# Hybrid decoder layer on one NeuronCore: key weights of the memory packed block by block, small loads behind them, the inverse in pieces, up-projections later

## The chip, the cores and the metric

One NeuronCore of a Trainium2 chip runs the whole program. The metric is the device time of that core in microseconds (us), as the median of the timed runs.

## What is computed

One step of a decoder layer for 320 tokens (256 of a prompt, 64 of a sample). Everything is fp32.

```python
xn = rmsnorm(x);  p = xn @ w_in        # 82 blocks of 128 columns: RWKV r, k, v, low-rank parts, SWA, memory q, gates
A  = rwkv7(p)          # 12 heads of 64: decay from tanh(low rank) @ up, delta rule, group norm, times g
B  = sliding_window_attention(p);  C = cross_attention(p, K(mem), V(mem))
K, V = rmsnorm(mem) @ w_mem_kv         # 256 tokens of memory
h  = x + rmsnorm((sum_i sigmoid(gate_i) * (o_i @ w_br_i)) @ w_o)
y  = h + rmsnorm((gelu(conv(z_gate)) * z_val) @ w_ffn_down)
```

## The kernel before

**Matmuls.** Each fp32 weight tile is split into a high part `wh` (a cast on ACT) and a low part `wl` (a subtraction on DVE), each fp32r. The activations are split too (`XH`, `XL`). One 128x128 weight tile costs three matmuls (`mm3`, L101 to L103): `wh` with `XH`, `wh` with `XL`, `wl` with `XH`. The text calls these three one k-step. A projection to 128 columns takes 16 k-steps over the 2048 inputs. Its weight comes in two chunks of 8 tiles (512 KB), and each chunk has one ACT cast (L356) and one DVE subtraction (L357, 128x1024).

**Opening stage.** The parameters `prm` are loaded first, as one transfer. Then nine blocks `KR` of the memory and of its key weights follow (`kload`, L197; `kprep`, L204): the first two hold one tile of 128 inputs, the others two. A block of key weights is gathered from four column tiles, so a partition gets four runs of 512 B or 1 KB. In `kprep` ACT casts the weight (L191), DVE or ACT makes `MH`, DVE makes `ML` (L215) and `wl` (L217), and PE multiplies into `psk`. Then come the value weights (`vload`, `vprep`, `vmm`), between them the RMS norm of `x`: `normed` (L253) takes the inverse norm `SX`, which ACT has copied out of PSUM (L304), and for each of 16 tiles DVE makes `xn` (L255), ACT casts it to `XH` (L256), POOL subtracts to `XL` (L257). The order on PE, ACT, DVE and POOL is that of the program text in this stage.

**RWKV stage.** A queue of projections (`push`, `prefetch`, `step`) gives PE its k-steps; weights are requested four chunks ahead and split two chunks ahead. Between k-steps the planner `pump` lets small threads issue their instructions. Its clock advances 0.405 per k-step, and a number that a thread yields is a pause on this clock. Three kinds of threads work on six head pairs `hp`: `early(hp)` (L487) does the up-projection of decay and `a` (L493, two matmuls into two buffers of the PSUM pool `pea`), a normalised key (L518 to L525), the scores (L544) and the products `AU` and `AP` (L601, copied by DVE at L602); `inverse(hp)` (L611) inverts blocks of 32 on DVE in one loop of pieces of 8; `late(hp)` (L653) solves, walks over the chunks (L724) and does the group norm: mean, variance (`rstd`, L129, then `rsv` on DVE, a power on POOL, `rex` on DVE at L138), spread back (L146), times `rn` (L760), gate up-projection (`psg`, L764) and product (L766). In this stage only PE keeps the order of the planner; the other engines' instructions are placed by a scheduler in the order in which they were issued, as they become ready. The pool `pea` (tag `sm`) has two buffers, so L493 must wait until both earlier tiles in it have been read.

**Later stages**: gates, attention, `w_o` and the ConvGLU, all k-steps; the change touches none of them.

Of the kernel before, what the change touches and what calls it, by code (L numbers as in the profile page):

```python
# [9 lines left out]
F32 = mybir.dt.float32  # L10
# [6 lines left out]
T = 320  # L17
# [9 lines left out]
HOP = 1.2  # L27
HV = (0, 1) * 8
TAIL = ((0, 1, 0), (11, 1, 1), (1, 2, 0), (3, 2, 0), (12, 1, 1), (5, 2, 0), (13, 1, 1), (7, 2, 0), (14, 1, 1), (9, 2, 0), (15, 1, 1))
E0 = 9.0  # L30
KKN, TRN_V, PRE = 3.2, 3.6, 4.8
NRM = (4, 3, 2)
UPQ = 7
RST = 2.5
SLV = 2.4
NI_LAT = 6.0
BLK_LAT = 6.0
IT_LAT = 8.0
SOFT = 3.5
SSOFT2, TRN2 = 9.0, 3.6  # L40
# [22 lines left out]
def tile_hybrid_step(ctx: ExitStack, tc: tile.TileContext, i, o):  # L63
    nc = tc.nc
# [35 lines left out]
    def mm3(ps, h, l, xh, xl, start, stop):  # L100
        PE.matmul(ps, h, xh, start=start, stop=False)  # L101
        PE.matmul(ps, h, xl, start=False, stop=False)  # L102
        PE.matmul(ps, l, xh, start=False, stop=stop)  # L103
# [37 lines left out]
    def spread(psum, ex, nh, tbs=TB):  # L141
        ps = psum.tile([128, 512], F32, tag="sm", name="sm")
        n = 0
        for j, (_, c0, c1) in enumerate(tbs):
            lhs = ex[:, j:j + 1].to_broadcast([128, 128]) if nh == 1 else ex[:, j, :]
            PE.matmul(ps[:, n:n + c1 - c0], lhs, C["ident"][:, c0:c1], start=True, stop=True)  # L146
            n += c1 - c0
        return ps[:, :n]
# [2 lines left out]
        A.copy(out=h, in_=src)  # L151
        V.tensor_sub(out=l, in0=src, in1=h.bitcast(F32))

    nc.sync.dma_start(out=prm, in_=i["param"])

    xst = ctx.enter_context(ExitStack())
    xp = xst.enter_context(tc.tile_pool(name="xp", bufs=1, side="left"))
# [10 lines left out]
    with tc.tile_pool(name="st", bufs=1, side="right") as st, tc.tile_pool(name="st2", bufs=3, side="right") as st2, \  # L168
# [12 lines left out]
        def load(dst, src):  # L181
            tc.keep_in_program_order(nc.sync.dma_start(out=dst, in_=src))
            return dst
# [13 lines left out]
        def kload(k0, kn):  # L197
            m2 = load(st2.tile([128, 2, 256], F32, tag="m2", name="m2", bufs=4)[:, :kn], i["memT"][:, k0:k0 + kn, :])
            r = raw(nq[0])[:, :512 * kn]
            nq[0] += 1  # L200
            load(r.rearrange("p (m c) -> p m c", m=4), i["wmk"][:, :, 128 * k0:128 * (k0 + kn)].rearrange("m p c -> p m c"))
            return m2, r

        def kprep(k0, kn, m2, r):  # L204
# [48 lines left out]
        def normed(k):  # L253
            t = st2.tile([128, T], F32, tag="xn", name="xn")
            V.scalar_tensor_tensor(out=t, in0=xf[:, k, :], scalar=col("g_pre", k), in1=SX, op0=ALU.mult, op1=ALU.mult)  # L255
            A.copy(out=XH[:, k, :], in_=t)  # L256
            G.tensor_sub(out=XL[:, k, :], in0=t, in1=XH[:, k, :].bitcast(F32))  # L257

        ld = [kload(*KR[q]) for q in range(3)]
        for q in range(9):  # L260
            if q + 3 < 9:
                ld.append(kload(*KR[q + 3]))
                if q == 3:
                    load(cst, i["const"])
            kprep(*KR[q], *ld[q])
        vr, vw = [], []

# [19 lines left out]
        xsquare(2)  # L287
        vmm(1)
        SM = st.tile([128, 256], F32, name="SM")
        SX = st.tile([128, T], F32, name="SX")  # L290
        sm = spread(smp, smt, 1, tbs=TB[:2])
        xsquare(3)
        A.copy(out=SM, in_=sm)
# [4 lines left out]
        vload(6)  # L298
        vprep(4)
        vmm(3, (0,))  # L300
        sx = spread(smp, xr, 1)
        vload(7)
        vprep(5)
        A.copy(out=SX, in_=sx)  # L304
        vmm(3, (1,))
        vmm(4)
        nk = 0
# [27 lines left out]

    def push(src, nk, xsel, done, ready=None):
        ch = [[src[:, k * 128:min(k + 8, nk) * 128], min(8, nk - k), None, None] for k in range(0, nk, 8)]
        jobs.append(dict(nk=nk, xs=xsel, done=done, ready=ready, ch=ch, k=0, ps=None))

    def prefetch():  # L340
        upcoming = []
# [18 lines left out]
    def step():  # L360
        if not jobs or (jobs[0]["ready"] is not None and not jobs[0]["ready"]()):
            return False
        j = jobs[0]
        k = j["k"]
        if k % 8 == 0:
            prefetch()
        if j["ps"] is None:
            j["ps"] = big.tile([128, 512], F32, tag="big", name="bigps")[:, :T]
        h, l = j["ch"][k // 8][3]
        xh, xl = j["xs"](k)  # L370
        js = slice((k % 8) * 128, (k % 8 + 1) * 128)
        mm3(j["ps"], h[:, js], l[:, js], xh, xl, k == 0, k == j["nk"] - 1)
        j["k"] += 1
        if j["k"] == j["nk"]:
            jobs.popleft()
            j["done"](j["ps"])
        return True

    def spawn(gen):
# [26 lines left out]
    with tc.tile_pool(name="rws", bufs=1, side="right") as rws, tc.tile_pool(name="rwp", bufs=2, side="right") as rwp, \  # L406
# [64 lines left out]
        def rw_done(hp, n, tix):  # L471
            def done(ps):
                rkv[hp, n] = rwt.tile([128, T], F32, tag="rkv", name="rkv", bufs=6)
                shifted(ps, tix, rkv[hp, n])
            return done
# [11 lines left out]
        def early(hp):  # L487
            cs = slice(hp * 128, hp * 128 + 128)
            yield lambda: "lora0" in state
            yield E0 if hp == 0 else 0.0  # L490
            psz, psa = (pea.tile([128, 512], F32, tag="sm", name="sm")[:, :T] for _ in range(2))
            for ps, rs in ((psz, slice(0, 64)), (psa, slice(64, 128))):
                PE.matmul(ps, lw[rs, 0, cs], lora[0][rs], start=True, stop=True)  # L493
# [104 lines left out]
            for c in range(10):  # L598
                for h in range(2):
                    r0, r1 = slice(64 * h + 32 * (c % 2), 64 * h + 32 * (c % 2) + 32), slice(64 * h + 32, 64 * h + 64)  # L600
                    PE.matmul(ps1[r0, c // 2, :], BT[r1, c, 96:128], AU[r1, c, 64:128], start=True, stop=True)  # L601
            V.tensor_copy(out=AP[:, :, 64:128], in_=ps1[:, 0:5])  # L602
            psb = pea.tile([128, 512], F32, tag="sm", name="sm")[:, :T]
            PE.matmul(psb, C["bones"], sr, start=True, stop=True)
            yield lambda: state["or"] >= hp - 1
# [5 lines left out]
        def inverse(hp, NI, it):  # L611
            yield lambda: state["inv"] == hp
            yield NI_LAT
            R = rw1.tile([128, 6, 32], F32, tag="R", name="R")
            W = rw1.tile([128, 6, 8], F32, tag="W", name="W")
            prod = rw1.tile([128, 576], F32, tag="prod", name="prod")
            NF = NI[0:120].rearrange("p j t -> p (j t)")
            for t in range(1, 8):
                nd = bass.AP(tensor=NF.tensor, offset=NF.offset + t, ap=[NF.ap[0], [264, 4], [0, t], [32, t]])
                pv = prod[0:120, 0:4 * t * t].rearrange("p (b i j) -> p b i j", i=t, j=t)  # L620
                V.tensor_mul(out=pv, in0=DI[0:120, :, 0:t, 0:t], in1=nd)
                V.tensor_reduce(out=DI[0:120, :, 0:t, t], in_=pv, axis=AX.X, op=ALU.add)
            yield 4.0
            for b in range(4):
                w = E[0:120, :, 0:8]
                if b:
                    nj = 8 * b
                    stp = 6 if b == 1 else 3
                    for i0 in range(0, 6, stp):
                        pv = prod[0:120, 0:stp * 8 * nj].rearrange("p (i t j) -> p i t j", t=8, j=nj)  # L630
                        V.tensor_mul(out=pv, in0=R[0:120, i0:i0 + stp, 0:nj].unsqueeze(2).to_broadcast([120, stp, 8, nj]),
                                     in1=NI[0:120, 0:nj, nj:nj + 8].rearrange("p j t -> p t j").unsqueeze(1).to_broadcast([120, stp, 8, nj]))
                        V.tensor_reduce(out=W[0:120, i0:i0 + stp, :], in_=pv, axis=AX.X, op=ALU.add)
                    w = W[0:120]
                    V.tensor_add(out=w, in0=w, in1=E[0:120, :, nj:nj + 8])
                pv = prod[0:120, 0:384].rearrange("p (i t j) -> p i t j", t=8, j=8)
                V.tensor_mul(out=pv, in0=w.unsqueeze(2).to_broadcast([120, 6, 8, 8]),
                             in1=DI[0:120, b].rearrange("p j t -> p t j").unsqueeze(1).to_broadcast([120, 6, 8, 8]))
                V.tensor_reduce(out=R[0:120, :, 8 * b:8 * b + 8], in_=pv, axis=AX.X, op=ALU.add)
                yield BLK_LAT  # L640
            sc2 = dsc.tile([20, 36, 32], F32, tag="sc2", name="sc2")
            nc.gpsimd.dma_start(out=sc2.rearrange("u i t -> (u i) t").rearrange("(p i) t -> p i t", i=6), in_=R[0:120])
            yield lambda: state["late"] >= hp - 1
            IT = its[hp % 2]
            for h in range(2):
                for q in range(2):
                    nc.gpsimd.dma_start(out=IT[64 * h + 32 * q:64 * h + 32 * q + 32, :, 32 * q:32 * q + 32],
                                        in_=sc2[10 * h + q:10 * h + 10:2, 0:32, :].rearrange("u j t -> j u t"))
            state["inv"] = hp + 1
            yield IT_LAT  # L650
            it[0] = IT
# [120 lines left out]
                yield from early(hp)  # L772

        fill = [(QKV, j, O_Q + j if j < 6 else O_K + j - 6) for j in range(10)] + [(MQ, j, O_MQ + j) for j in range(4)]
        for j in range(2):
            push(i["win"][O_LORA + j], 16, xs, lora_done(j))
        for hp in range(6):
            for n, nm, tix in ((1, "k", 6 + hp), (0, "r", hp), (2, "v", 12 + hp)):
                push(i["win"][O_RW + 3 * hp + n], 16, xs, rw_done(hp, nm, tix))
            for _ in range(FILL[hp]):  # L780
                dst, j, mt = fill.pop()
                push(i["win"][mt], 16, xs, fill_done(dst, j))
# [367 lines left out]
    with tc.tile_pool(name="ff", bufs=1, side="left") as ff, tc.tile_pool(name="fft", bufs=2, side="left") as fft, \  # L1150
# [6 lines left out]
        j = 0  # L1157
# [210 lines left out]
```

## Time and profile before

| | |
|---|---|
| runs | 2054.89, 2054.66, 2051.91 us; median 2054.66 |
| profiled execution | 2050.91 us, its span 2049.1 us |
| PE busy | 1988.0 us (97%), mean granted clock 0.987 |
| DVE, ACT, POOL busy | 1226.4, 821.6, 203.1 us |
| read from HBM | 293.53 MB, mean 148 GB/s |

The profiled execution lies 3.75 us under the median. Its time is 1.8 us more than its span, the time around the first and the last instruction. Busy times add up over the program and say little of one stage; the waits of an engine and the chosen stretches of time (below) show where PE stood.

### The profile page before, as it was taken

How to read it: one execution, taken by the hardware profiler on the slowest of the kernel's cores; microseconds unless marked ns; L12 is line 12 of the kernel's file. 1: busy time of each engine (PE TensorE's matmuls, PEld its weight loads, DVE VectorE, ACT ScalarE, POOL GpSimd, SP SyncE). 2: the span in 40 equal slices, each digit the busy share in tenths (PEclk: the TensorE clock that was granted, in tenths of full speed). 3: DMA queues.
4: the chain of work that ended last, by engine and by line, in shares of the span. 5: the costliest groups of instructions: out<-in, count | busy, mean ns of one | idle time of the engine just before them, and what ended most of it. 6: DMA issues, size and time to landing. Idle time of an engine off the chain costs nothing.

```text
span 2049.1 us, 36434 instructions
## 1 busy us (share of the span) xinstructions
PE 1988.0 (97%) x14923; PEld 1929.5 (94%) x14923; DVE 1226.4 (60%) x2048; ACT 821.6 (40%) x1306; POOL 203.1 (10%) x452
## 2 busy tenths in 40 slices
PE   7999898989999999999999999999999999999997
PEld 7888797889998999999999999999999999999997
DVE  7788777875457754444547653555555555455456
ACT  5533443433443433333445443433343333334235
POOL 4511231121200000000100100000000000000001
PEclk9999999999999999999999999999999999999999
DMA  7533343334545444544553444445444444444443
GB/s 272 171 127 101 108 126 93 104 111 128 193 162 164 139 129 150 161 150 154 194 173 116 141 151 148 152 159 181 145 153 148 151 151 148 151 148 155 145 139 127
DMA packets 93000, 303.28 MB, mean 148 GB/s; under 512 B 11356, under 2 KB 17654, under 8 KB 92816
## 3 DMA queue, kind: packets, MB, share of 16 engines
q1 hardware_dynamic: 83232, 273.42, 40.2%
q0 software_dynamic: 8880, 26.71, 3.9%
q8 instruction: 117, 1.92, 0.4%
q10 hardware_dynamic: 720, 0.82, 0.1%
q14 instruction: 51, 0.42, 0.1%
HBM read 293.53 MB, written 9.34 MB: 148 GB/s over the span
## 4 chain that ended last, share of the span: by engine, by line
PE 60%; issue 5%; POOL 1%; DVE 0%; ACT 0%; POOLq 0%; DVEq 0%
PE bigps L101 19%; PE bigps L102 19%; PE bigps L103 19%; PE bigps L1139 0%; PE bigps L1137 0%; PE bigps L1140 0%; POOL yacc L1227 0%; POOL merged L1062 0%; POOL yacc L1228 0%; DVE MG L813 0%; PE sm L146 0%; PE sm L870 0%; POOL rsr L1087 0%; PE psos L1021 0%; PE sm L1212 0%
## 5 line engine op out<-in xcount | busy, mean ns | idle before, releaser
L101 PE MATMUL bigps<-XH,wh 128*128 128x320 f32 x2656 | 843.6, 318 | 1.0 <-ACT gt L830 0.5
L103 PE MATMUL bigps<-XH,wl 128*128 128x320 f32 x2656 | 824.8, 311 | 2.1 <-DVE wl L357 2.1
L102 PE MATMUL bigps<-XL,wh 128*128 128x320 f32 x2656 | 825.0, 311 | 1.6 <-POOL XL L257 1.5
L97 DVE TENSOR_TENSOR wl<-raw,wh 128x1024 fp32r<-128x1024 f32 (+1 forms) x299 | 357.4, 1196 | 275.7 <-ACT wh L96 275.4
L101 PEld LDWEIGHTS bigps<-XH,wh 128*128 128x128 f32 x2656 | 502.4, 189 | 17.4 <-issue 12.7
L96 ACT CAST wh<-raw 128x1024 fp32r<-128x1024 f32 (+1 forms) x299 | 306.4, 1025 | 519.6 <-PE bigps L102 396.2
L102 PEld LDWEIGHTS bigps<-XL,wh 128*128 128x128 f32 x2656 | 502.7, 189 | 4.1 <-POOL XL L257 2.4
L103 PEld LDWEIGHTS bigps<-XH,wl 128*128 128x128 f32 x2656 | 502.1, 189 | 2.6 <-DVE wl L357 2.6
L357 DVE TENSOR_TENSOR wl<-raw,wh 128x1024 fp32r<-128x1024 f32 (+2 forms) x212 | 245.2, 1157 | 197.4 <-ACT wh L356 193.8
L356 ACT CAST wh<-raw 128x1024 fp32r<-128x1024 f32 (+2 forms) x212 | 208.3, 983 | 304.5 <-PE bigps L102 251.6
L102 PE MATMUL bigps<-fl,wh 128*128 128x320 f32 x704 | 217.5, 309 | 0.0
L101 PE MATMUL bigps<-fh,wh 128*128 128x320 f32 x704 | 217.4, 309 | 0.0
L103 PE MATMUL bigps<-fh,wl 128*128 128x320 f32 x704 | 217.4, 309 | 0.0
L101 PEld LDWEIGHTS bigps<-fh,wh 128*128 128x128 f32 x704 | 132.2, 188 | 0.2 <-ACT fh L151 0.2
L102 PEld LDWEIGHTS bigps<-fl,wh 128*128 128x128 f32 x704 | 132.2, 188 | 0.1
L103 PEld LDWEIGHTS bigps<-fh,wl 128*128 128x128 f32 x704 | 132.2, 188 | 0.0
L1196 DVE TENSOR_TENSOR yacc<-yacc,bigps 128x320 f32<-128x320 f32 x80 | 38.9, 487 | 84.1 <-PE bigps L103 84.0
L1170 POOL COPY cout<-zp 128x9 f32<-128x9 f32 x88 | 15.4, 205 | 731.6 <-DVE zp L1167 731.6
L101 PE MATMUL bigps<-MG,wh 128*128 128x320 f32 x208 | 64.4, 309 | 0.3 <-ACT MG L812 0.3
L103 PE MATMUL bigps<-MG,wl 128*128 128x320 f32 x208 | 64.3, 309 | 0.0
L102 PE MATMUL bigps<-MG,wh 128*128 128x320 f32 x208 | 64.3, 309 | 0.0
L1166 DVE TENSOR_TENSOR zp<-bigps,S 128x256 f32<-128x256 f32 x44 | 18.7, 425 | 56.7 <-PE bigps L103 56.7
(404 smaller groups left out, 2367.9 us busy)
## 6 DMA issues: line engine op xcount, KB each, us to landing
raw<-in_wup SPq DMA_DIRECT2D x176, 512.0 KB, 3.5
raw<-in_win SPq DMA_DIRECT2D x164, 512.0 KB, 3.6
raw<-in_wdn SPq DMA_DIRECT2D x80, 512.0 KB, 3.2
raw<-in_wo SPq DMA_DIRECT2D x32, 512.0 KB, 3.7
raw<-in_wbr_rw SPq DMA_DIRECT2D x16, 384.0 KB, 3.3
raw<-in_wbr_sw SPq DMA_DIRECT2D x16, 384.0 KB, 3.1
ck<-in_cmk POOLq DMA_DIRECT2D x8, 512.0 KB, 4.7
cv<-in_cmv POOLq DMA_DIRECT2D x8, 512.0 KB, 3.7
```

Of the source, the lines that this page charges most:

```text
L96: A.copy(out=h, in_=raw)
L97: V.tensor_sub(out=l, in0=raw, in1=h.bitcast(F32))
L101: PE.matmul(ps, h, xh, start=start, stop=False)
L102: PE.matmul(ps, h, xl, start=False, stop=False)
L103: PE.matmul(ps, l, xh, start=False, stop=stop)
L356: A.copy(out=h, in_=c[2])
L357: V.tensor_sub(out=l, in0=c[2], in1=h.bitcast(F32))
L1166: V.tensor_mul(out=zp[:, 2:258], in0=psz[:, 0:TP], in1=S2[:, 0:TP])
L1170: G.tensor_copy(out=cout[:, j, :, e], in_=zp[:, 256 + e:337 + e:10])
L1196: V.tensor_add(out=yacc[:, m, :], in0=yacc[:, m, :], in1=ps)
```

## The change

1. Parameters: only their first 32 columns (the gains of the two norms) are loaded ahead of the key weights; the other columns and the constants go behind the ninth block of them.
2. The host packs the key weights block by block, so that one block is one run of 2 KB or 4 KB per partition.
3. `SX` stays in PSUM. The subtraction to `XL` of tiles 2, 5, 8, 11 and 14 goes from POOL to DVE, one tile later.
4. The first low-rank projection and the first key projection alternate chunk by chunk (`push_pair`).
5. `E1`: the up-projection of `hp` 1 to 5 pauses 5.0 on the planner's clock; before, it had no pause. The copy of `AP` goes from DVE to ACT.
6. `RST`, the pause between variance and spread, is 3.4 and was 2.5.
7. The inverse pauses after `t` of 4 and of 7 and after each off-diagonal piece (2.4), and 3.0 instead of 6.0 after each block.

```diff
-E0 = 9.0
+E0, E1 = 9.0, 5.0
 KKN, TRN_V, PRE = 3.2, 3.6, 4.8
 NRM = (4, 3, 2)
 UPQ = 7
-RST = 2.5
+RST = 3.4
 SLV = 2.4
 NI_LAT = 6.0
-BLK_LAT = 6.0
+PIECE, BLK_LAT = 2.4, 3.0
...
-    nc.sync.dma_start(out=prm, in_=i["param"])
+    nc.sync.dma_start(out=prm[:, 0:32], in_=i["param"][:, 0:32])
...
-            load(r.rearrange("p (m c) -> p m c", m=4), i["wmk"][:, :, 128 * k0:128 * (k0 + kn)].rearrange("m p c -> p m c"))
+            load(r, i["wmk"][:, 512 * k0:512 * (k0 + kn)])
             return m2, r
...
             A.copy(out=XH[:, k, :], in_=t)
+            if k % 3 == 2:
+                low.append((k, t))
+                return
+            if low:
+                k1, t1 = low.pop()
+                V.tensor_sub(out=XL[:, k1, :], in0=t1, in1=XH[:, k1, :].bitcast(F32))
             G.tensor_sub(out=XL[:, k, :], in0=t, in1=XH[:, k, :].bitcast(F32))
+
+        low = []
 
         ld = [kload(*KR[q]) for q in range(3)]
         for q in range(9):
             if q + 3 < 9:
                 ld.append(kload(*KR[q + 3]))
-                if q == 3:
+                if q == 5:
                     load(cst, i["const"])
+                    load(prm[:, 32:], i["param"][:, 32:])
...
             kprep(*KR[q], *ld[q])
         vr, vw = [], []
 
...
-        SX = st.tile([128, T], F32, name="SX")
...
-        sx = spread(smp, xr, 1)
+        SX = spread(smp, xr, 1)
         vload(7)
         vprep(5)
-        A.copy(out=SX, in_=sx)
         vmm(3, (1,))
         vmm(4)
         nk = 0
...
     def push(src, nk, xsel, done, ready=None):
         ch = [[src[:, k * 128:min(k + 8, nk) * 128], min(8, nk - k), None, None] for k in range(0, nk, 8)]
-        jobs.append(dict(nk=nk, xs=xsel, done=done, ready=ready, ch=ch, k=0, ps=None))
+        jobs.append(dict(nk=nk, xs=xsel, done=[done], ready=ready, ch=ch, k=0, ps=[None]))
+
+    def push_pair(srcs, xsel, dones):
+        ch = [[src[:, k * 128:(k + 8) * 128], 8, None, None] for k in (0, 8) for src in srcs]
+        jobs.append(dict(nk=32, xs=xsel, done=dones, ready=None, ch=ch, k=0, ps=[None, None]))
 
...
-        if j["ps"] is None:
-            j["ps"] = big.tile([128, 512], F32, tag="big", name="bigps")[:, :T]
+        nl = len(j["ps"])
+        q, kk = k // 8 % nl, k // (8 * nl) * 8 + k % 8
+        if j["ps"][q] is None:
+            j["ps"][q] = big.tile([128, 512], F32, tag="big", name="bigps")[:, :T]
         h, l = j["ch"][k // 8][3]
-        xh, xl = j["xs"](k)
+        xh, xl = j["xs"](kk)
         js = slice((k % 8) * 128, (k % 8 + 1) * 128)
-        mm3(j["ps"], h[:, js], l[:, js], xh, xl, k == 0, k == j["nk"] - 1)
+        last = kk == j["nk"] // nl - 1
+        mm3(j["ps"][q], h[:, js], l[:, js], xh, xl, kk == 0, last)
         j["k"] += 1
         if j["k"] == j["nk"]:
             jobs.popleft()
-            j["done"](j["ps"])
+        if last:
+            j["done"][q](j["ps"][q])
         return True
...
             yield lambda: "lora0" in state
-            yield E0 if hp == 0 else 0.0
+            yield E0 if hp == 0 else E1
...
-            V.tensor_copy(out=AP[:, :, 64:128], in_=ps1[:, 0:5])
+            A.copy(out=AP[:, :, 64:128], in_=ps1[:, 0:5])
...
                 pv = prod[0:120, 0:4 * t * t].rearrange("p (b i j) -> p b i j", i=t, j=t)
                 V.tensor_mul(out=pv, in0=DI[0:120, :, 0:t, 0:t], in1=nd)
                 V.tensor_reduce(out=DI[0:120, :, 0:t, t], in_=pv, axis=AX.X, op=ALU.add)
-            yield 4.0
+                if t in (4, 7):
+                    yield PIECE
...
                         V.tensor_mul(out=pv, in0=R[0:120, i0:i0 + stp, 0:nj].unsqueeze(2).to_broadcast([120, stp, 8, nj]),
                                      in1=NI[0:120, 0:nj, nj:nj + 8].rearrange("p j t -> p t j").unsqueeze(1).to_broadcast([120, stp, 8, nj]))
                         V.tensor_reduce(out=W[0:120, i0:i0 + stp, :], in_=pv, axis=AX.X, op=ALU.add)
+                        yield PIECE
                     w = W[0:120]
...
-        for j in range(2):
-            push(i["win"][O_LORA + j], 16, xs, lora_done(j))
         for hp in range(6):
-            for n, nm, tix in ((1, "k", 6 + hp), (0, "r", hp), (2, "v", 12 + hp)):
-                push(i["win"][O_RW + 3 * hp + n], 16, xs, rw_done(hp, nm, tix))
+            three = [(O_RW + 3 * hp + n, rw_done(hp, nm, tix)) for n, nm, tix in ((1, "k", 6 + hp), (0, "r", hp), (2, "v", 12 + hp))]
+            if hp == 0:
+                push_pair((i["win"][O_LORA], i["win"][three[0][0]]), xs, [lora_done(0), three[0][1]])
+                push(i["win"][O_LORA + 1], 16, xs, lora_done(1))
+                three = three[1:]
+            for mt, done in three:
+                push(i["win"][mt], 16, xs, done)
...
     wmk = mtiles(np.asarray(w_mem_kv)[:, :512])
+    wmk = A(np.concatenate([wmk[:, :, 128 * k:128 * (k + n)].transpose(1, 0, 2).reshape(128, 512 * n)
+                            for k, n in [(0, 1), (1, 1)] + [(k, 2) for k in range(2, 16, 2)]], 1))
```

PE at the end of `early` of the second head pair and the start of the third one's. L601 and L604 are the last products of `early`, L493 the up-projection, L724 one step of the walk over chunks. Before:

```order
L601 MATMUL sm<-AU,BT 32x64 x20
L604 MATMUL sm<-rkv,cst 128x320
L493 MATMUL sm<-lora_755,lw 128x320 [waits DVE_49] x2
L101 MATMUL bigps<-XH,wh 128x320
L102 MATMUL bigps<-XL,wh 128x320
L103 MATMUL bigps<-XH,wl 128x320
L724 MATMUL psb<-SA,AB 128x64 [waits Activation_49]
```

After the change (L616, L619, L508 and L741 are the same instructions). Between L619 and L508 stand thirteen k-steps and four steps of the walk; the first k-step and one step of the walk are shown:

```order
L616 MATMUL sm<-AU,BT 32x64 x12
L619 MATMUL sm<-rkv,cst 128x320
L101 MATMUL bigps<-XH,wh 128x320
L102 MATMUL bigps<-XL,wh 128x320
L103 MATMUL bigps<-XH,wl 128x320
...
L741 MATMUL psb<-SA,AB 128x64 [waits Activation_49]
...
L508 MATMUL sm<-lora_754,lw 128x320 [waits PE_49]
L508 MATMUL sm<-lora_754,lw 128x320 [waits DVE_49]
```

The up-projection moved from directly behind L604 to 13 k-steps behind it.

DVE at the same place: the inverse (L637 to L633), then the copy of `AP` and the product `bonus`. Before:

```order
L637 TENSOR_TENSOR prod<-rcst 120x384 [waits DVE_49]
L639 TENSOR_REDUCE R<-prod 120x6x8 [waits DMASW1_49,DVE_49]
L631 TENSOR_TENSOR prod<-R,NI 120x384 [waits DVE_49]
L633 TENSOR_REDUCE W<-prod 120x48 [waits DVE_49]
L602 COPY AP<-sm 128x5x64 [waits PE_49]
L607 TENSOR_TENSOR bonus<-sm,rkv 128x320 [waits PE_49]
```

After:

```order
L654 TENSOR_TENSOR prod<-rcst 120x384 [waits DVE_49]
L656 TENSOR_REDUCE R<-prod 120x6x8 [waits DMASW1_49,DVE_49]
L647 TENSOR_TENSOR prod<-R,NI 120x384 [waits DVE_49]
L649 TENSOR_REDUCE W<-prod 120x48 [waits DVE_49]
L622 TENSOR_TENSOR bonus<-sm,rkv 128x320 [waits PE_49]
```

The copy has left DVE's order; `bonus`, which frees the other `pea` buffer, still stands behind the same four instructions.

DVE at the end of `late` of the first head pair: `rex`, the chain of the next pair's normalised key (L519 to L524, in the changed kernel L534 to L539), the product with `rn` (L760, L777). Before:

```order
L138 COPY rex<-rsr 128x384 [waits Pool_49]
L530 SCALAR_TENSOR_TENSOR ar<-rt 128x320 [waits Activation_49]
L760 TENSOR_TENSOR rp<-rp,sm 128x320 [waits DVE_49,PE_49]
L357 TENSOR_TENSOR wl<-raw,wh 128x1024 [waits DMAHW7_49,Activation_49]
L765 TENSOR_TENSOR rp<-rp,bonus 128x320 [waits Activation_49]
L519 TENSOR_SCALAR sm<-sm 128x320 [waits DVE_49,PE_49]
L522 TENSOR_SCALAR rt<-rt,hka,hw 128x320
L520 RECIPROCAL sm<-sm 128x320 [waits DVE_49]
```

After:

```order
L138 COPY rex<-rsr 128x384 [waits Pool_49]
L368 TENSOR_TENSOR wl<-raw,wh 128x1024 [waits DMAHW0_49,PE_49,Activation_49]
L534 TENSOR_SCALAR sm<-sm 128x320 [waits PE_49]
L537 TENSOR_SCALAR rt<-rt,hka,hw 128x320
L535 RECIPROCAL sm<-sm 128x320 [waits DVE_49]
L538 TENSOR_TENSOR rt<-rt,rkv 128x320 [waits DVE_49]
L539 SCALAR_TENSOR_TENSOR rt<-rt 128x320
L777 TENSOR_TENSOR rp<-rp,sm 128x320 [waits PE_49]
```

The product with `rn` moved from ahead of the weight split and the reciprocal to behind both.

## Rows read from the trace of the kernel before

**Rows 1.** The page: busy time, share and instructions of each engine.

```profile
PE 1988.0 (97%) x14923; PEld 1929.5 (94%) x14923; DVE 1226.4 (60%) x2048; ACT 821.6 (40%) x1306; POOL 203.1 (10%) x452
```

**Rows 2.** Waits of PE, 100 to 452 us.

```profile
PE sm L493 <- DVE AP L602: 13.9, 5, 3.8
PE sm L146 <- DVE rex L138: 6.0, 4, 4.2
...
PE sm L764 <- DVE rp L760: 1.9, 1, 1.9
PE sm L493 <- ACT rt L495: 1.2, 2, 0.6
...
PE sm L544 <- DVE rp L766: 0.8, 1, 0.8
```

**Rows 3.** Timeline around 188 us: DVE, then PE.

```profile
187.84 0.48 DVE L602 COPY AP<-sm 128x320 f32<-128x320 f32 x1
188.37 1.83 PE L493 MATMUL sm<-lora,lw 64*128 64x320 f32 x4 [3.78 <-DVE AP L602]
```

**Rows 4.** Seven stretches at half clock: length, busy, PEclk, DMA share, GB/s.

```profile
76.80:80.20 3.40, 3.40 (x14) 3.40 (x14) 2.26 (x2) 1.86 (x4) 3.40 (x9) 0.50 0.90 344
...
sum 44.20, PE 37.51 PEld 32.25 DVE 34.17 ACT 13.11 POOL 3.40; mean PE 5.36 PEld 4.61 DVE 4.88 ACT 1.87 POOL 0.49
```

**Rows 5.** Timeline of PE, two starts at full clock, two at half.

```profile
65.58 0.31 PE L101 MATMUL bigps<-XH,wh 128*128 128x320 f32 x1
65.73 0.31 PE L102 MATMUL bigps<-XL,wh 128*128 128x320 f32 x1
...
128.19 0.47 PE L102 MATMUL bigps<-XL,wh 128*128 128x320 f32 x1
128.45 0.47 PE L103 MATMUL bigps<-XH,wl 128*128 128x320 f32 x1
```

**Rows 6.** Stretches: one head pair, and all that is left from 450 us.

```profile
223.47:295.82 72.35, 66.79 (x625) 60.37 (x625) 54.04 (x101) 28.23 (x58) 16.44 (x28) 0.93 0.36 109
450.00:2030.00 1580.00, 1574.92 (x11365) 1551.62 (x11366) 862.76 (x1409) 624.33 (x926) 73.69 (x249) 1.00 0.45 152
```

**Rows 7.** Waits of PE, 0 to 100 us: us in total, times, longest.

```profile
PE psk L101 <- ACT wh L191: 6.2, 1, 6.2
PE psk L103 <- DVE wl L217: 3.5, 3, 1.3
PE bigps L103 <- DVE wl L357: 2.1, 1, 2.1
PE bigps L102 <- POOL XL L257: 1.5, 2, 1.1
```

**Rows 8.** Start of the span, ACT (timeline: start, length; in brackets the wait).

```profile
5.49 0.62 ACT L191 CAST wh<-raw 128x512 fp32r<-128x512 f32 x1 [3.46 <-DMA raw<-in_wmk]
10.35 1.04 ACT L191 CAST wh<-raw 128x1024 fp32r<-128x1024 f32 x1 [2.75 <-DMA raw<-in_wmk]
```

**Rows 9.** DMA packets of 8 to 16 us, then of 32 to 44 us.

```profile
DMA packets 2452, 2.87 MB, mean 359 GB/s; under 512 B 118, under 2 KB 1981, under 8 KB 2452
DMA packets 1240, 4.92 MB, mean 410 GB/s; under 512 B 140, under 2 KB 140, under 8 KB 1239
```

**Rows 10.** Timeline of DVE and POOL, 62 to 72 us.

```profile
62.67 1.47 DVE L255 SCALAR_TENSOR_TENSOR xn<-xf,prm,SX 128x320 f32<-128x320 f32 x3
66.04 3.33 DVE L255 SCALAR_TENSOR_TENSOR xn<-xf,prm,SX 128x320 f32<-128x320 f32 x3 [0.76 <-POOL XL L257]
63.79 8.11 POOL L257 TENSOR_TENSOR XL<-xn,XH 128x320 fp32r<-128x320 f32 x6 [1.62 <-ACT XH L256]
```

**Rows 11.** DVE operations by shape, 100 to 450 us: busy us, mean ns, idle before.

```profile
L765 DVE TENSOR_TENSOR rp<-rp,bonus 128x320 f32<-128x320 f32 x4 | 1.9, 486 | 0.7 <-ACT rp L761 0.7
L760 DVE TENSOR_TENSOR rp<-rp,sm 128x320 f32<-128x320 f32 x4 | 1.9, 485 | 2.2 <-PE sm L146 2.2
```

**Rows 12.** Timeline of DVE, 354 to 358 us.

```profile
354.55 2.15 DVE L520 RECIPROCAL sm<-sm 128x320 f32<-128x320 f32 x1
```

## The prediction, made before the changed kernel was run

> **What bounds the kernel now.** I read the page first, then the waits of PE, then the granted clock by stretches, then the timelines around the longest waits.
>
> The page gives PE 1988.0 us of work in a span of 2049.1 and DVE 1226.4 [rows 1]. So PE sets the time, and a change can gain only where PE stands or runs slowly. From 450 us to 2030 us PE is busy for 1574.92 of 1580.00 us at clock 1.00 [rows 6]: nothing is to be had there, and the change leaves that part alone. All that can move lies before 450 us.
>
> Between 100 and 452 us the waits of PE have one large row: the up-projection L493 waits five times, 13.9 us, for the copy of `AP` on DVE, and twice, 1.2 us, for ACT [rows 2]. The timeline shows why: DVE starts the copy at 187.84 and PE's L493 follows at 188.37 after 3.78 us of standing [rows 3]; ahead of the copy DVE was working through the inverse. Next come `rex` with 6.0 us, then the gate up-projection L764 (1.9) and the scores L544 (0.8), both behind the product with `rn` [rows 2]. These six entries that the change touches make 13.9 + 1.2 + 6.0 + 1.9 + 0.8 = 23.8 us (L493 counts twice, once for each releaser).
>
> The waits cost more than their length. In seven stretches of together 44.2 us the granted clock is 0.50, and PE is busy for 37.5 us of them [rows 4]; each begins at or just behind a wait of PE. At full clock two matmuls start 0.15 us apart, at half clock 0.26 [rows 5], so 1 - 0.15/0.26 = 42% of that busy time is lost. The first stretch (3.40 us, all busy) loses 1.4 us, the other six (37.5 - 3.4 = 34.1 us) lose 14.3 us.
>
> Before 100 us PE waits 6.2 us for the first weight, 3.5 for `wl` of the key blocks, then 2.1 for `wl` and 1.5 for `XL` at the start of the projections [rows 7].
>
> **The change part by part.** The profiled execution took 2050.91 us, 1.8 more than its span and 3.75 less than the median of the runs; the sum is made against it.
>
> *Start.* ACT waits 3.46 us for the first key weight and 2.75 us for the third [rows 8]. The parameters are 159 KB, of which 143 KB move back; at 359 GB/s [rows 9] that is 0.4 us. Packed blocks replace runs of 512 B and 1 KB by 2 and 4 KB. With mostly small packets the queues moved 359 GB/s, with larger ones 410 [rows 9], so the 1.5 MB up to the third block (two of 384 KB and one of 768 KB, with their memory tiles; 4.3 us at 359) take 0.5 us less. Together 0.9 us. Behind the third block DVE's `wl` is late [rows 7], so the gain grows no further. Bounds: 0, if DVE is late from the start, and 2, if part of the 3.5 us goes as well. The parameters and constants that now stand later in SP's queue are ahead of the value weights; without cover that costs those 0.4 us.
>
> [...]
>
> *Norm of x, 62 to 76 us.* Sixteen subtractions on POOL take 8.11/6 = 1.35 us each while DVE works; `xn` on DVE takes 3.33/3 = 1.11 us beside them, and 1.47/3 = 0.49 in the group that began before POOL did [rows 10]. Five leave POOL, 6.8 us; they add five times 0.49 to 1.11 us to DVE. With `push_pair`, tiles 8 to 15 are needed eight k-steps later: three matmuls of 0.15 us [rows 5], so 0.45 us a step, 3.6 us in all. That covers the 1.5 us of waits on `XL`. The wait of 2.1 us on `wl` depends on DVE, which gets more subtractions and less slowed `xn`; I leave half, 1.1. So 2.5 us, and with the wait the clock stretch of 1.4 goes: 3.9. Bounds: 1 (the wait on `wl` stays or grows) and 5.
>
> [...] On this chip a 128x320 product takes 485 ns with an operand in PSUM and 486 without [rows 11], so the sum keeps nothing for it.
>
> *Up-projection.* It moves 13 k-steps, 13 x 0.45 = 5.8 us, behind the products. Both `pea` buffers must be read by then. The longest wait was 3.8 us [rows 2], so 5.8 covers it, and the copy no longer queues behind the inverse but goes to ACT, which is 40% busy [rows 1]. 13.9 + 1.2 = 15.1 us go. Late next could be the decay chain on DVE and ACT up to the scores: it still has 27 k-steps, 12 us, in the first pair and 40 or more, 18 us, in the others; I cost that at nothing.
>
> *Variance to spread.* `RST` gives `rex` two k-steps more, and the inverse in pieces shifts the solve by 4 to 14 k-steps. That changes which DVE work stands ahead of the end of each pair. For the first and second pair the product with `rn` now stands behind a weight split and the reciprocal. The reciprocal alone takes 2.15 us [rows 12]. Before, one pair had this order, and PE waited 1.9 + 0.8 = 2.7 us there [rows 2]; two pairs make 5.4. For the third and fourth pair no row shows the new order; the bounds are 0 and 4.2, the longest wait for `rex` [rows 2], and I take 2.1 each, 4.2. Against 6.0 + 1.9 + 0.8 = 8.7 before, this part ends at 9.6.
>
> *Inverse in pieces.* No instruction is added; DVE takes weight splits and chain work in between. The last gate up-projection comes 16 k-steps, 7 us, later; over a hundred k-steps of other projections lie between it and the first use of its result, so it costs nothing. For DVE's lateness elsewhere I put 2.5 us of new waits (0 to 6; the upper end is all of today's `rex` row).
>
> Waits of this stage: 15.1 + 8.7 - 9.6 - 2.5 = 11.7 us gained.
>
> *Clock.* Of 14.3 us lost I leave 4.3, three stretches of 3.4 us at 42%, since waits of 2 to 3 us remain. Behind L764's wait of 1.9 us no slow stretch follows; behind most longer ones it does. Gain 10.0; bounds 0 and 14.3.
>
> **Sum:** 0.9 + 3.9 + 11.7 + 10.0 = 26.5 us; 2050.9 - 26.5 = 2024.4. Against the median it would be 3.75 higher; I stay with 2024.
>
> **Rivals.**
>
> *DVE becomes the bound.* The longest pair takes 72.35 us, PE is busy 66.79, DVE 54.04 [rows 6]. Without waits and slow clock a pair would take some 57 us, 95% of it DVE's, and any wait of DVE would show on PE as waits for `wl`. For it: this ratio. Against: DVE's splits run two chunks, 16 k-steps or 7 us, ahead. Half of the stage's gain is then lost: 0.9 + 3.9 + 5.9 + 5.0 = 15.7, 2035 us.
>
> *The clock still falls.* The waits go as computed, but the new ones of 2 to 3 us bring as much slow time: 26.5 - 10.0 = 16.5, 2034 us. For it: all seven stretches follow waits, some short. Against: the 1.9 us that were followed by none.
>
> *Nearly everything goes.* The new waits are 4 us instead of 12.1 and no slow stretch is left: 0.9 + 5 + 19.8 + 14.3 = 40, 2011 us.
>
> *Slower: the pairs do not shorten.* DVE stands for 18.3 us of the longest pair (72.35 - 54.04). If that is latency of its own chains and not time in which it waits for PE, the pairs keep their length and the waits behind the reciprocal come on top: 2.7 us each and a slow stretch of 3.4 to 6.8 us, about 2.1 at 42%, in five pairs 24 us; less 4.8 for the opening, 2070 us. It decides once DVE lags by more than the 7 us of its lead. Against: PE is the one that waits for a queue behind the inverse, and the change takes it out.
>
> *It does not do what it says.* Packing and the smaller first load may be hidden by DVE's pace: only 0.9 us less, 2025.
>
> **How the numbers follow.** A measurement of this kernel can tell about 0.2%, 4 us, from no change. Chances: forecast 0.57 (the hidden start within it), DVE the bound 0.13, clock 0.11, nearly everything 0.10, slower 0.09 (a tenth of this would end near zero). The first four are faster; I take off 0.05 for gains that end within 4 us of zero. Faster 0.86, same 0.06, slower 0.08. The range reaches from 2008, below the best case, to 2042, above the two weaker ones; outside lie the slower case and the tails.
>
> **What would show it.** Right: the up-projection's row among PE's waits is under 2 us; at the first two pairs PE waits 2 to 3 us for the product with `rn`; the first key weight is cast before 5.1 us; stretches at half clock between 100 and 450 us sum to under 15 us; DVE is over 85% busy in the middle pairs; from 450 us on nothing changes but the start. Wrong: waits on `wl` of over 5 us together between 100 and 450 us, or slow stretches as long as before, or a wait for `XL` or `wl` of over 2 us at the first projections.

## The result, and the profile after

The changed kernel takes 2034.18 us (median of 4 runs, 2032.29 to 2035.56) against 2053.91 for the kernel before (4 runs, one of them new). The ratio is 0.9905 with a 95% interval of 0.9887 to 0.9922, so 0.8 to 1.1% faster. The forecast was 2024 us, its range 2008 to 2042: the sign and the range held, the size did not. The profiled execution took 2033.18 us, 17.7 less than the profiled one before; the sum of the forecast, which was made against that one, was 26.5, half as much again.

The page after, span and busy times; against [rows 1], PE is busy 8 us less for the same 14923 matmuls:

```profile
span 2031.3 us, 36435 instructions
## 1 busy us (share of the span) xinstructions
PE 1980.1 (97%) x14923; PEld 1924.5 (95%) x14923; DVE 1222.4 (60%) x2047; ACT 823.0 (41%) x1311; POOL 195.3 (10%) x447
```

PE's waits after, 100 to 452 us (us in total, times, longest), to be read against [rows 2]; L616 was L601, L741 was L724, L706 was L689, L559 was L544, L781 was L764:

```profile
PE psb L741 <- ACT SA L743: 4.9, 2, 2.8
PE sm L616 <- DVE AU L609: 3.3, 3, 1.8
PE sm L559 <- DVE ar L548: 3.2, 2, 1.8
PE sm L706 <- ACT AU L691: 2.9, 2, 1.8
PE sm L129 <- ACT rp L771: 2.9, 2, 1.5
PE sm L559 <- DVE rp L783: 2.4, 2, 1.2
PE sm L781 <- DVE rp L777: 2.4, 2, 1.8
PE sm L616 <- ACT AU L609: 1.5, 3, 0.6
PE sm L146 <- ACT BT L594: 1.1, 1, 1.1
PE sm L559 <- DVE rp L777: 0.8, 1, 0.8
PE sm L768 <- ACT rp L764: 0.4, 1, 0.4
PE sm L533 <- ACT rt L521: 0.3, 1, 0.3
```

Of the same view before, [rows 2] leaves out the rows of the solve (L689), `AU` (L601) and `ar` (L533):

```profile
PE sm L689 <- ACT AU L674: 1.9, 2, 1.7
...
PE sm L601 <- ACT AU L594: 1.2, 2, 0.6
...
PE sm L544 <- DVE ar L533: 0.8, 2, 0.4
PE sm L601 <- DVE AU L594: 0.7, 3, 0.3
```

The row of the up-projection is gone, 15.1 us. But the view adds up to 26.1 us, where before it was 28.4. Rows that did not exist (the walk, L741; the variance, L129) or were small (`AU`, `ar`) have taken its place. No wait is longer than 2.8 us; the longest before was 4.2.

Two stretches with nearly the same work, from just behind the first head pair's scores to the 700th k-step, first of the kernel before, then after (length, PE busy, PEld, DVE, ACT, POOL, clock, DMA):

```profile
110.97:548.62 437.65, 408.96 (x3850) 378.17 (x3849) 325.73 (x593) 174.49 (x354) 87.70 (x157) 0.95 0.38 117
```

```profile
105.36:529.90 424.54, 399.98 (x3836) 371.98 (x3835) 319.61 (x578) 174.37 (x354) 79.73 (x143) 0.98 0.38 117
```

It is 13.1 us shorter. PE's busy time fell by 9.0 us and its idle time by only 4.1 (28.7 to 24.6). The largest part of what was gained here is clock: the five stretches at half clock after sum to 20.4 us, where [rows 4] has 40.8 without its first. At the 42% that the forecast takes for lost, 14.3 us became 8.6, 5.7 less; the rest of the 9.0 holds, among other things, the 14 matmuls fewer of the stretch after.

One of the five, and their sum:

```profile
201.10:204.50 3.40, 3.40 (x15) 3.40 (x15) 2.38 (x5) 3.34 (x7) 2.88 (x7) 0.51 0.30 102
...
sum 20.40, PE 20.40 PEld 18.24 DVE 14.57 ACT 8.29 POOL 5.36; mean PE 4.08 PEld 3.65 DVE 2.91 ACT 1.66 POOL 1.07
```

How far ahead of the kernel before the changed one is, by the start of the same k-step: 1.7 us at the first, 7.6 behind the 20th, 5.6 behind the 80th, 18.7 behind the 700th, 17.85 at the end. The last 0.9 us are no loss by waiting: behind the 700th k-step PE waits less than before (3.0 against 3.6 us), but it also has the 14 matmuls of the attention to do that stood ahead of that k-step before.

At the opening the wait for the first weight stays; beside it only small waits are left, and the wait for `XL` in [rows 7] is gone:

```profile
PE psk L101 <- ACT wh L191: 5.4, 2, 5.1
PE psk L103 <- DVE wl L217: 1.6, 3, 0.8
...
PE bigps L103 <- DVE wl L368: 0.4, 1, 0.4
```

The timelines show why (DVE, then POOL): three `xn` take 1.45 us, and POOL is no longer behind. `xn` reads `SX` in PSUM now; compare the 3.33 us in [rows 10].

```profile
64.37 1.45 DVE L255 SCALAR_TENSOR_TENSOR xn<-xf,prm,sm 128x320 f32<-128x320 f32 x3
```

```profile
65.47 2.70 POOL L263 TENSOR_TENSOR XL<-xn,XH 128x320 fp32r<-128x320 f32 x2 [0.29 <-ACT XH L256]
```

The new wait on the walk, timeline of ACT and then PE. ACT stands 2.94 us at the exponential L524, which needs from DVE the subtraction behind the scan (L515); the weight cast and the walk's copy `SA` stand behind it, and PE stands for `SA`:

```profile
317.29 0.47 ACT L524 ACTIVATE rt<-rt 128x320 f32<-128x320 f32 x1 [2.94 <-DVE rt L515]
317.66 1.03 ACT L367 CAST wh<-raw 128x1024 fp32r<-128x1024 f32 x1
318.60 0.31 ACT L743 ACTIVATE SA<-psb,pc 128x64 f32<-128x64 f32 x1
```

```profile
318.96 0.43 PE L741 MATMUL psb<-SA,AB 128*128 128x64 f32 x2 [2.05 <-ACT SA L743]
```

### The profile page after: what moved, and what is told of

It is laid out like the page before. It is cut to its first block, busy times and chain, and to the rows that moved or that the text cites. A ratio compares the mean times of both kernels' runs of the same rounds, so it can differ in the third digit from the quotient of the medians.

```text
span 2031.3 us, 36435 instructions
## 1 busy us (share of the span) xinstructions
PE 1980.1 (97%) x14923; PEld 1924.5 (95%) x14923; DVE 1222.4 (60%) x2047; ACT 823.0 (41%) x1311; POOL 195.3 (10%) x447
## 4 chain that ended last, share of the span: by engine, by line
PE 57%; issue 5%; POOL 1%; DVE 0%; ACT 0%; POOLq 0%; DVEq 0%
PE bigps L101 19%; PE bigps L103 18%; PE bigps L102 18%; PE bigps L1159 0%; PE bigps L1157 0%; PE bigps L1160 0%; POOL merged L1082 0%; POOL yacc L1247 0%; POOL yacc L1248 0%; DVE MG L833 0%; PE sm L146 0%; POOL rsr L1107 0%; PE sm L1232 0%; PE sm L1100 0%; PE sm L1235 0%
## 5 line engine op out<-in xcount | busy, mean ns | idle before, releaser
L1186 DVE TENSOR_TENSOR zp<-bigps,S 128x256 f32<-128x256 f32 x44 | 18.7, 425 | 57.2 <-PE bigps L103 57.2
```

Source lines behind the costliest of these rows:

```text
L1186: V.tensor_mul(out=zp[:, 2:258], in0=psz[:, 0:TP], in1=S2[:, 0:TP])
```

## Experiments

Ratios are to the kernel before, run on the same chip in the same rounds. The changed kernel is at 0.9905. A profile is one execution, and executions of one kernel differ: the run with the exponentials behind the walk took 2031.42 to 2041.28 us. A microsecond between two profiles shows little by itself.

| run | ratio | 95% interval |
|---|---|---|
| packing alone | 1.0003 | 0.9990 to 1.0015 |
| parameter load alone | 0.9996 | 0.9985 to 1.0006 |
| norm, projections in the old order | 0.9998 | 0.9987 to 1.0009 |
| norm, projections alternating | 0.9981 | 0.9969 to 0.9992 |
| later up-projection, `AP` copy on ACT | 0.9957 | 0.9943 to 0.9972 |
| inverse in pieces alone | 0.9979 | 0.9968 to 0.9991 |
| changed, exponentials behind the walk | 0.9923 | 0.9904 to 0.9942 |
| changed, inverse with its old pauses | 0.9963 | 0.9950 to 0.9977 |
| changed, inverse without off-diagonal part | 0.9819 | 0.9801 to 0.9837 |
| changed, no pause ahead of the up-projection | 0.9910 | 0.9893 to 0.9928 |
| changed, inverse's products on POOL | 0.9967 | 0.9952 to 0.9982 |
| changed, copies out of PSUM on ACT | 0.9896 | 0.9880 to 0.9913 |

### The opening, part by part

**Packing alone**, the kernel before with

```diff
-load(r.rearrange("p (m c) -> p m c", m=4), i["wmk"][:, :, 128 * k0:128 * (k0 + kn)].rearrange("m p c -> p m c"))
+load(r, i["wmk"][:, 512 * k0:512 * (k0 + kn)])
```

and the host's packing. Expected:

> The kernel before with the packed key weights alone. By the forecast's sum: packets grow, the third block's cast (10.35 us before) comes 0.4 to 0.6 us earlier, the first projection matmul (64.81 before) up to 0.5 earlier, the span 0.5 shorter. [...]

The third block's cast starts at 9.88 us, 0.47 earlier, the first projection matmul 0.48 earlier; 8 to 16 us move faster than the 359 GB/s of [rows 9]:

```profile
DMA packets 1166, 3.19 MB, mean 399 GB/s; under 512 B 130, under 2 KB 130, under 8 KB 1166
```

The rate holds in every profile: 351 to 363 GB/s in the six kernels that gather their key weights, 365 to 399 in the eight with packed blocks. The forecast's half microsecond came out in this one profile, but it is not shown to come from the packing. The third cast lies between 10.21 and 10.84 us in the five kernels with the opening loads of before, and between 9.90 and 10.96, median 10.56, in the seven that load as the changed kernel does. In the whole time nothing can be seen.

**Parameter load alone**, `prm` in two parts, constants behind the ninth block. Expected:

> The kernel before with the split parameter load alone. By the forecast's sum: the first key weight's cast (5.49 before) 0.4 us earlier, the first projection matmul 0.4 earlier. If the whole 1.0 us by which the changed kernel's first matmul came earlier belongs to this part: 0.9 to 1.1 earlier, and the packing shows nothing.

The first cast comes at 4.76 us, 0.73 earlier, but the first projection matmul 0.25 later than before. In this run the clock fell to half from 13.9 to 17.3 us, in the key blocks: their matmuls start 0.21 us apart there and 0.12 behind it. Together in the changed kernel the two parts bring the first cast to 4.46 us (5.49 in [rows 8]). This is larger than the spread: 4.46 to 4.75 us in the seven kernels with these loads, 5.10 to 5.52 in the five with those of before.

**Norm of x** without and with alternation:

```diff
-sx = spread(smp, xr, 1)
+SX = spread(smp, xr, 1)
-A.copy(out=SX, in_=sx)
...
+            if k % 3 == 2:
+                low.append((k, t))
+                return
```

> The kernel before with SX left in PSUM and every third XL on DVE, the projections in their old order. If POOL's rate made the waits of 62 to 76 us: XL waits (1.5 us) and the wl wait (2.1) both under 0.5 and the 3.4 us at half clock gone, 4 to 5 us less, as much as with alternation. If the old order of need made them: XL or wl waits of 1.5 us or more stay and at most 2.5 us are gained.

> As the run before it, with the two first projections alternating. By the changed kernel's trace: no XL wait, wl wait near 0.4, no slow stretch at 77 us, k-step 20 some 5.5 to 6 us earlier than in the kernel before, of which 1 to 3 are lost again before the first scores (their wait for ar grows from 0.4 to about 1.8). The forecast had 3.9 us for it.

In the old order PE still waits 1.3 us for `XL` and 0.8 for `XH`, as in the second case of the expectation. The lead over the kernel before is 2.6 us behind the 20th k-step, of which 1.2 were there at the first. With alternation it is 7.1 behind the 20th and 5.7 behind the 80th. The alternation carries most of it, and part is given back at the first scores, as in the changed kernel.

### Up-projection and inverse

**Later up-projection alone**: the kernel before with

```diff
-            yield E0 if hp == 0 else 0.0
+            yield E0 if hp == 0 else E1
...
-            V.tensor_copy(out=AP[:, :, 64:128], in_=ps1[:, 0:5])
+            A.copy(out=AP[:, :, 64:128], in_=ps1[:, 0:5])
```

> The kernel before with the later up-projection and the AP copy on ACT alone. Forecast: the up-projection's waits fall from 15.1 us to under 1, no new wait of over 2 us, time at half clock from 41 to under 15 us, 20 to 26 us less. Rival, ACT's order: the exponentials of the decay now stand ahead of the walk's copies on ACT and wait there for the scan on DVE; PE then waits 3 to 6 us on the walk (L724) and some 10 us are gained at most.

The rival's number came: 9 us by the ratio. The up-projection's waits are gone, and PE waits as long as before (28.6 us against 28.4), most of it at three other places. What fell is the time at half clock, from 41 to 27 us:

```profile
PE sm L146 <- DVE rex L138: 8.0, 3, 4.0
PE psb L724 <- ACT SA L726: 5.9, 2, 3.0
PE sm L129 <- ACT rp L754: 4.7, 2, 4.2
```

**Inverse in pieces alone**: the new pauses (`PIECE`, `BLK_LAT`) in the kernel before, `RST` unchanged.

> The kernel before with the inverse in pieces alone. Forecast: no instruction more, so within 2 us of before, the up-projection's waits still 10 us or more. Rival 1: the pieces let the AP copy through, the up-projection's waits fall under 7 us, 8 to 15 us less. Rival 2: the pieces stand ahead of other chains, PE's waits on DVE's AU, ar and rp copies grow by 4 us or more, 4 to 10 us more time.

It gains 4 us (2 to 7 by the interval), more than nothing and less than rival 1. The up-projection still waits 12.0 us, while the wait for `rex` fell from 6.0 to 0.8, with `RST` as it was:

```profile
PE sm L493 <- DVE AP L602: 12.0, 5, 4.2
PE sm L766 <- DVE rp L762: 3.1, 2, 1.9
...
PE sm L146 <- DVE rex L138: 0.8, 1, 0.8
```

**Changed kernel, inverse with its old pauses:**

> The changed kernel with the inverse's old pauses. If the pieces are what delays the scan and AU on DVE: PE's waits on AU (L616 row, 3.3) and on the walk (4.9) fall by half or more, time 3 to 8 us less than the changed kernel. If the pieces are what makes room for the later up-projection: waits grow by 5 us or more and the time with them, 5 to 12 us more.

The second case: some 12 us slower than the changed kernel by the ratios. `rex`, the walk and the variance wait again, and 34.1 us run at half clock instead of 20.4:

```profile
PE psb L739 <- ACT SA L741: 6.0, 2, 3.0
PE sm L129 <- ACT rp L769: 4.8, 2, 4.2
PE sm L146 <- DVE rex L138: 3.6, 1, 3.6
```

So the pieces, which the forecast put at nothing, are worth 0.6% in the changed kernel, beside all its other parts. The longer `RST` and the copy of `AP` on ACT were not tried alone, so what each adds stays open.

**Changed kernel, no pause** (`E1` at 0, the copy still on ACT):

> The changed kernel with the up-projection directly behind the products again (E1 at 0), the AP copy still on ACT. If the pause is what took the 15 us of waits away: the up-projection waits 8 us or more again (for bonus on DVE, the other buffer), the walk's wait of 4.9 goes, 4 to 12 us more time. If moving the copy to ACT was enough: under 3 us of waits at the up-projection and no more time than the changed kernel.

The waits did what the first case says: the up-projection waits 9.5 us for `bonus`, the reader of the other buffer, and the walk's wait falls from 4.9 to 1.6:

```profile
PE sm L508 <- DVE bonus L622: 9.5, 5, 4.1
...
PE psb L741 <- ACT SA L743: 1.6, 1, 1.6
```

The time did not: 0.9910 against 0.9905, intervals that cover each other. The pause moves the waits and takes none away: PE's sum to 24.7 us without it, to 26.1 with it. So the changed kernel's gain does not need the pause; the norm with alternation (4 us alone) and the pieces (4 us alone) explain less than half of it one by one, and the rest belongs to parts that work together or were not tried alone.

### What stands behind the new waits

**Exponentials behind the walk.** In the changed kernel the three exponentials are issued behind the walk and pinned there on ACT:

```diff
-            A.activation(out=eLe, in_=x1, func=AF.Exp, scale=-C2)
...
             yield lambda: state["late"] >= hp - 1 and clock[0] >= ready
+            for out, in_, sg in ((eLe, x1, -C2), (eL, L, -C2), (emL, L, C2)):
+                tc.keep_in_program_order(A.activation(out=out, in_=in_, func=AF.Exp, scale=sg))
```

> The changed kernel with the decay's three exponentials issued and pinned behind the walk on ACT; the planner's order on PE is the same. If ACT standing at their head (16.8 us, five times) makes the walk's waits: ACT's row for the exponentials falls under 3 us, PE's wait on the walk from 4.9 to 3 or less (the 2.8 us one has the key's copy ahead of it and stays), 2 to 6 us less than the changed kernel. If DVE's lateness alone makes them: the walk's waits stay at 4 to 5 us, no difference beyond 1 us.

In the changed kernel ACT stands 16.8 us at the exponentials:

```profile
ACT rt L524 <- DVE rt L515: 16.8, 5, 4.8
```

These are gone, yet PE waits at the walk and the variance no less than before (8.4 us against 7.8), and the kernel is not faster. ACT now stands at another instruction that needs DVE, the scaled copy of the key (ACT's row, then PE's):

```profile
ACT rt L520 <- DVE rkv L471: 10.6, 3, 4.7
```

```profile
PE sm L129 <- ACT rp L771: 4.4, 2, 3.1
PE psb L741 <- ACT SA L743: 4.0, 1, 4.0
```

So the order of the exponentials on ACT alone is not the cause. That DVE's lateness behind it is, as the second case says, fits these rows but is not shown by them.

**Inverse without its off-diagonal part**, pauses kept; this leaves out the products and sums between blocks:

```diff
-                        V.tensor_mul(out=pv, in0=R[0:120, i0:i0 + stp, 0:nj].unsqueeze(2).to_broadcast([120, stp, 8, nj]),
...
-                        V.tensor_reduce(out=W[0:120, i0:i0 + stp, :], in_=pv, axis=AX.X, op=ALU.add)
                         yield PIECE
```

> The changed kernel without the off-diagonal products and sums of the inverse: five multiplications and five reductions a head pair less on DVE, 8 us of about 54; the pauses and PE's order stay (the inverse, and so the RWKV output, is left incomplete). If DVE's load is what PE waits for: PE's waits between 100 and 452 us fall from 26 to under 13, time at half clock from 20 to under 10 us, 10 to 18 us less than the changed kernel. If single late chains or ACT's order make the waits: they stay at 20 us or more, under 6 us less.

0.9819, some 18 us less than the changed kernel by the ratios (12.5 by the two profiled executions). PE's waits fall to 16.6 us, the half clock to 13.7, not quite as far as expected. DVE is busy 246.59 us of 350, in the changed kernel 291.37 (the changed kernel, then this run):

```profile
100.00:450.00 350.00, 325.15 (x3160) 300.55 (x3161) 291.37 (x542) 144.09 (x301) 69.70 (x129) 0.97 0.37 114
100.00:450.00 350.00, 333.43 (x3296) 309.06 (x3297) 246.59 (x471) 148.85 (x311) 76.99 (x137) 0.98 0.40 119
```

**The products on POOL**: `G.tensor_mul` in place of `V.tensor_mul` in the off-diagonal piece.

> The changed kernel with the five off-diagonal multiplications of the inverse on POOL: DVE gets 5 us a head pair back, but each product comes 0.6 to 1.0 us later. If DVE's load rules: PE's waits between 100 and 452 us fall by 5 us or more, 4 to 10 us less than the changed kernel. If the inverse's own length rules, or DVE slows beside POOL as at the norm of x: waits at the solve (L706, L616) grow, no gain or up to 8 us more.

0.9967, some 13 us slower than the changed kernel. Between 100 and 450 us DVE is busy 34 us less, but stands 28.0 us at its next instruction, waiting for POOL, whose products take 1663 ns instead of 1022:

```profile
L649 DVE TENSOR_REDUCE W<-prod 120x24 f32<-120x384 f32 (+2 forms) x28 | 17.4, 620 | 28.0 <-POOL prod L647 28.0
```

**Copies out of PSUM on ACT**: the four places with `A.copy if h else V.tensor_copy` become `A.copy`.

> The changed kernel with the DVE half of the copies out of PSUM (BT, AP, AU at two places; some 28 us on DVE over six head pairs) moved to ACT, PE's order the same; nothing is left out. The run without the off-diagonal sums took 50 us of DVE work away for 0.9% of the time, so if DVE's load rules, 28 us are worth some 7 to 10 us: 2024 to 2028 us, PE's waits for AU on DVE gone, total waits from 26 to under 20. If ACT's queue takes over as the late one: waits for ACT copies (AU, SA, AP) grow by as much, within 3 us of the changed kernel or slower.

No difference (0.9896). DVE has 25.8 us less to do, and ACT and DVE now wait for each other, ACT at the exponential, DVE for a copy behind it:

```profile
ACT rt L524 <- DVE rt L515: 31.1, 5, 7.1
```

```profile
DVE rkv L469 <- ACT rkv L466: 34.6, 8, 6.9
```

So DVE's busy time alone is not the bound. It helps to take work out of the inverse where it stands ahead of the scan, `AU` and the group norm in DVE's order; it did not help to take 25.8 us from elsewhere, which ACT then had to do, or to leave DVE standing at the same place. Whether the gain without the off-diagonal part is due to the load or to the shorter run of work ahead of those chains was not tried apart and stays open.

## Why the prediction was right, and where it was not

- **Start, 0.9 us: too large.** Measured 1.7 at the first projection matmul. But the norm part alone gave 1.2 at the same point, which the forecast counted under the next term, so 0.5 is left for the start. In the seven profiles with the changed opening the first projection matmul lies at 63.11 to 63.99 us, with the norm part alone at 63.57 and 63.65: the start is worth 0.5 us at most. The first cast did come earlier, by more than the forecast's 0.4; it was not carried through to PE's projections.
- **Norm of x, 3.9 us.** From the first projection matmul (1.7 ahead) to the 80th k-step (5.6 ahead) 3.9 were gained: 5.9 by the 20th k-step, then 2.0 back. That the sum comes out to the tenth is luck, as its parts do not: the wait on `wl` fell to 0.4, not 1.1, and the first scores lost 1.4 (their wait for `ar` grew from 0.4 to 1.8).
- **PSUM operand.** No cost showed, as [rows 11] said (it sets a product beside a sum of the same shape): three `xn` from PSUM take 1.45 us, where from SBUF three took 1.47 us in the group that began before POOL did and 3.33 beside POOL [rows 10].
- **Waits of the head pairs, 11.7 us: the step that failed.** (The 23.8 us it starts from are five entries, not six; the sum is right.) Of it, "15.1 us go" held at its place, and the waits at the end of the pairs, put at 9.6, came to 2.4 + 2.4 + 0.8 + 1.1 = 6.7: at the first two pairs 3.0 and 1.9 us for the product with `rn` and the scores behind it, where 2.7 each was forecast. What failed is "for DVE's lateness elsewhere I put 2.5 us of new waits". The waits on the walk, the variance, `AU`, `ar` and the solve sum to 18.7 us, against 4.6 for the same places before: 14 us instead of 2.5. PE idled 4.1 us less, not 11.7. The run with the later up-projection alone shows it: the same 28 us of waits at other places. The forecast had asked what would be late next, named the decay chain up to the scores and put it at nothing. But the wait for `ar` grew to 3.2 us, and ACT, standing for the chain's result, holds up the walk, 4.9 us.
- **Up-projection, "5.8 covers it".** True, and worth little: without the pause the time is the same within the intervals.
- **Inverse in pieces, put at no gain.** It is worth 4 us alone and some 12 us in the changed kernel. The forecast saw that no instruction is added and did not ask what the whole blocks kept waiting.
- **Clock, 10.0 us.** PE's busy time fell by 9.0 in the stretch, of which the time at half clock explains 5.7 by the forecast's own 42%. The gain came, the forecast's size is somewhat too large: 20.4 us ran at half clock, and the forecast had drawn the line at 15 and left 10.2. That waits bring the clock down is the forecast's reading of seven stretches and not shown apart: with the later up-projection alone the waits stayed (28.6 us) and the time at half clock fell to 27.
- **Sum.** 5.6 up to the 80th k-step (forecast 4.8), 4.1 of waits (11.7), 9.0 of busy time (10.0), less 0.9 for the work that moved behind the stretch: 17.8.
- **Rivals.** "DVE becomes the bound" gave 2035 us, and 2034 came. Its mechanism is near but not the same: PE never waits for `wl` between 100 and 452 us, and moving work off DVE did not help. "The clock still falls" gave 2034, but its mechanism is out: the time at half clock was halved, from 40.8 to 20.4 us. That both numbers fit is coincidence; the slower case is out by every run.
- **Signs named.** The up-projection under 2 us, the first cast before 5.1 us, and no wait over 2 us on `XL` or `wl`: as forecast. DVE over 85% busy in the middle pairs: missed, 291.37 of 350 us, 83%. Half clock under 15 us: missed, 20.4. PE waits 2 to 3 us for the product with `rn` at the first two pairs: L781 waits twice, 1.8 and 0.6 us, and with the scores it comes to the 3.0 and 1.9 above.

## What to carry to other kernels

A wait that is read at one place shows how far another engine is behind; moving the waiting instruction shows the next place in the order, so price it by what the late engine still has to do first, and by who stands behind it in other queues. Long runs of work with no one waiting (here the inverse, 12 us of the changed kernel's time) are worth cutting into pieces between the chains that someone does wait for. Waits that move can pay through the clock even where their sum stays: with the later up-projection alone it went from 28.4 to 28.6 us, the time at half clock from 41 to 27. Which waits bring the clock down was not tried.

## What was not expected of the hardware

The clock in the opening differed between kernels with the same opening code. With the norm part alone PE's granted clock was full at 9.7 us and at half from 13.1, for 6.8 us; PE waited 1.16 and 1.56 us there (the run's stretches: length, PE busy, PEld, DVE, ACT, POOL, clock, DMA):

```profile
9.70:13.10 3.40, 1.59 (x11) 1.18 (x10) 1.29 (x4) 2.00 (x4) 0.20 (x1) 1.00 1.08 375
13.10:19.90 6.80, 5.90 (x27) 5.90 (x28) 6.73 (x8) 4.94 (x8) 5.99 (x6) 0.50 1.04 357
```

Six of the twelve experiments fell like this between 12 and 15 us; the kernel before and the changed one did not: their granted clock is 1.00 from 5 to 20 us, though their key matmuls start 0.21 us apart up to 11.75 and 16.65 us, as at half clock in the run with the parameter load alone, and 0.12 behind that. Four of the six have the opening of the changed kernel, and so have two experiments that did not fall, so neither the earlier loads nor the norm part decides it; what does stays open. It cost little: the first projection matmul came at 63.31 to 63.99 us in those four, at 63.11 to 63.61 in the changed kernel and the two others.
